# The first group of a Mamba-2 input projection, regrouped by token tile

## The chip, the cores and the metric

The kernel runs on one NeuronCore of a Trainium2 chip. The metric is the device time of one execution in microseconds (us); a time given for a kernel is the median of several runs. A core has five engines that run side by side, each through its own list of instructions in order: TensorE (PE, matrix products and transposes, with results in PSUM), VectorE (DVE), ScalarE (ACT), GpSimd (POOL) and SyncE (SP, which issues the transfers here). They wait for one another through semaphores. The compiler's list of an engine is fixed when the kernel is built, so an instruction that waits holds up everything behind it on its engine.

## The reference, cut to what matters

The kernel computes one step of a decoder trunk of two layers: a Mamba-2 layer (SSD), then a multi-head latent attention layer (MLA), each with a residual, and a final norm. 1024 prompt rows and 8 x 8 sample rows pass through together as T = 1088 rows. Only the entry of the SSD layer matters here:

```python
def rms_norm(x, w):
    xf = x.astype(F32)
    y = xf * lax.rsqrt(jnp.mean(xf * xf, axis=-1, keepdims=True) + NORM_EPS)
    return (y * w.astype(F32)).astype(x.dtype)

def ssd_mixer(h, conv_buf, ssm_state, w_in, conv_w, conv_b, dt_bias, a_log, d_skip, norm_w, w_out):
    proj = jnp.einsum('btd,de->bte', h, w_in)
    z = proj[..., :SSD_D_INNER]
    xbc = proj[..., SSD_D_INNER:SSD_D_INNER + SSD_CONV_DIM]
    dt_raw = proj[..., SSD_D_INNER + SSD_CONV_DIM:]
    xbc, new_buf = causal_conv(xbc, conv_buf, conv_w, conv_b)
    xbc = jax.nn.silu(xbc.astype(F32))
...
    dt = jax.nn.softplus(dt_raw.astype(F32) + dt_bias.astype(F32))
    a_head = -jnp.exp(a_log.astype(F32))
    y, new_state = ssd_scan(xs, dt, a_head, bm, cm, ssm_state.astype(F32))
    y = y + d_skip.astype(F32)[:, None] * xs
    y = y.reshape(b, t, SSD_D_INNER) * jax.nn.silu(z.astype(F32))
```

Here h is the normalised x, z the gate, and xbc holds x, B and C; a norm by group and the product with w_out follow. D_MODEL is 1024, the inner width 2048, and there are 8 groups of 4 heads. Group g needs two columns of 128 for B and C, two of 128 for x, and 256 columns of z; dt has 32 columns for all groups. The decay needs cumulative sums of dt over chunks of 128 rows.

## The kernel before

Products are made from numbers split in two: `split` (line 128) rounds a tile to a high part on ACT and subtracts it on DVE for a low part, and every product is three matmuls, high x high, high x low and low x high. So the rows x are kept normalised and turned as `xh` and `xl` (feature by token), and each weight as `wih` and `wil`.

After a first part for group 0, a loop over the groups g = 1..7 (`ssd_groups`, line 1138) runs 21 steps t per group: a projection piece of group g (`Flow.proj`) beside the scan of group g-1 (`Scan`). In this loop the order on every engine is the order in which the program issues (`manual_schedule`). In the first part before, a scheduler orders the instructions of each engine. The MLA layer behind it is touched by nothing here.

The first part before, `layer_ssd` (lines 1250 to 1309), works so:

- `norm_steps` (line 244) takes the 9 tiles of 128 rows (the last has the 64 sample rows) in three column groups of 384, 384 and 320 rows. `norm_rows` (line 208) loads x, squares it on ACT with a sum per row, takes the root on DVE and POOL (`rstd_of`) and scales the rows on DVE; `norm_cols` (line 229) turns them on PE, and ACT and DVE split them into `xh` and `xl`, with the norm weight as a factor per partition.
- Beside it `Group.pair(0, True)` projects B and C for each column group as its rows come (line 418); then `pair(1)` projects the two x blocks. `Group.block` (line 443) copies each piece to `raw` (two buffers), and convolves the whole block: one ACT instruction (line 466) and three on DVE (line 469).
- `load_zdt` (line 318) loads and splits the weights of z and dt on POOL, and `Group.gates` (line 489) then projects z and dt tile by tile (line 500, 24 matmuls of 288 columns for a tile).
- `ssd_dt` (line 336) makes the decays once dt of all tiles is there: an ACT chain (lines 346 to 348) of |x|, exp and log with table loads between, DVE (350, 352), PE sums (358, 359), transposes (381), and stores to DRAM (388) from where `load_decay` (689) reads the decay rows `M` of a chunk.
- `ssd_groups` then starts with `front(0)` (four PE instructions) and `front1(0)` of the scan, whose ACT work (line 734) waits for `M`. The first matmul of the loop's third projection piece (t = 2 of g = 1) follows `back(0)` of the scan.

SP issues transfers in order; a transfer is issued only when an earlier one on the same of eight semaphores has landed. PSUM has two banks each for the transposes (`tr`) and the projections (`pj`).

Of the kernel before, what the change touches and what calls it, by code (L numbers as in the profile page):

```python
# [9 lines left out]
F32 = mybir.dt.float32  # L10
# [7 lines left out]
D = 1024  # L18
# [126 lines left out]
def ssd_tiles(k):  # L145
# [13 lines left out]
    nc.sync.dma_start(k.alog, k.I["ssd_a_log"][0].partition_broadcast(128))  # L159
    nc.scalar.activation(k.alog, k.alog, AF.Exp)  # L160
# [3 lines left out]
def ssd_consts(k):  # L164
# [7 lines left out]
    nc.sync.dma_start(k.dtb, I["ssd_dt_bias"][0].partition_broadcast(128))  # L172
# [3 lines left out]
def load_vectors(k, vp, psum):  # L176
    nc, I, cp = k.nc, k.I, k.cp
    if True:
        r1 = vp.tile([128, 128], F32, name="r1")
        nc.sync.dma_start(r1, I["ssd_conv_w"].rearrange("o k (b c) -> (o k b) c", c=128))  # L180
        r2 = vp.tile([68, 128], F32, name="r2")
        nc.sync.dma_start(r2[0:16], I["norm_w"].rearrange("l (b c) -> (l b) c", c=128))
        nc.sync.dma_start(r2[16:48], I["ssd_conv_b"].rearrange("o (b c) -> (o b) c", c=128))
        nc.sync.dma_start(r2[48:64], I["ssd_norm_w"].rearrange("o (b c) -> (o b) c", c=128))
        nc.sync.dma_start(r2[64:68], I["mla_q_norm_w"].rearrange("o (b c) -> (o b) c", c=128))
        k.vec = cp.tile([128, 196], F32, name="vec")
        p = psum.tile([128, 512], F32, tag="tr", name="vecp", bufs=PB["tr"])
        nc.tensor.transpose(p[:, :128], r1, k.ident)
        nc.tensor.transpose(p[:, 128:196], r2, k.ident[:68, :68])
        nc.vector.tensor_copy(k.vec, p[:, :196])  # L190
    k.convw = [k.vec[:, 32 * j : 32 * j + 32] for j in range(4)]
    k.normc = [k.vec[:, 128:136], k.vec[:, 136:144]]
    k.convb = k.vec[:, 144:176]
    k.ssdn = k.vec[:, 176:192]
    k.qn = k.vec[:, 192:196]

# [106 lines left out]
def conv_state_T(k, pool, psum):  # L303
    nc, I = k.nc, k.I
    r = k.sqp("cst")[:96]
    src = I["state_conv"].rearrange("o b w c -> (o b w) c")
    for q in range(4):
        nc.sync.dma_start(r[24 * q : 24 * q + 24], src[:, 1024 * q : 1024 * q + 1024])
    for half in range(2):
        p = psum.tile([128, 512], F32, tag="tr", name=f"cvp{half}", bufs=PB["tr"])  # L310
# [5 lines left out]


def load_zdt(k, pool):
    nc = k.nc
    w = k.I["ssd_w_in"][0].rearrange("(k p) e -> p k e", p=128)  # L320
    k.wzd = []
    k.dtr = pool.tile([128, 9, H], F32, name="dtr")
    nc.gpsimd.memset(k.dtr[64:, 8], 0.0)
    for j in range(2):
        ks = slice(4 * j, 4 * j + 4)
        hi = pool.tile([128, 4, 288], F32R, name=f"zdh{j}")
        lo = pool.tile([128, 4, 288], F32R, name=f"zdl{j}")
        raw = load_raw(pool, 4, 288, 1)
        nc.sync.dma_start(raw[:, :, 0:256], w[:, ks, 0:256])
        nc.sync.dma_start(raw[:, :, 256:288], w[:, ks, DIN + CONV :])  # L330
        nc.gpsimd.tensor_copy(hi, raw)
        nc.gpsimd.tensor_tensor(lo, raw, hi.bitcast(F32), op=ALU.subtract)
        k.wzd += kslices((hi, lo), 4)


def ssd_dt(k, pool, psum):
# [5 lines left out]
    alog = k.alog  # L342
    x = k.dtr.rearrange("p i h -> p (i h)")
# [10 lines left out]
    af = a.rearrange("p i h -> p (i h)")  # L354
    pa = psum.tile([128, 512], F32, tag="y", name="dpa", bufs=PB["y"])
    pt = psum.tile([128, 512], F32, tag="pv", name="dpt", bufs=PB["pv"])
    for p, l, ls in ((pa, k.masku, k.masks), (pt, ones, blks)):
        nc.tensor.matmul(p[:, 0:256], l, af[:, 0:256], start=True, stop=True)
        nc.tensor.matmul(p[:, 256:288], ls, af[:64, 256:288], start=True, stop=True)
    acs = pool.tile([128, n], F32, name="acs")  # L360
# [17 lines left out]
    nc.scalar.activation(k.decp, pt[:, :256].rearrange("p (i h) -> p h i", h=H), AF.Exp)  # L378
    p = psum.tile([128, 512], F32, tag="tr", name="acsp", bufs=PB["tr"])
# [2023 lines left out]
```

## Time and profile before

| | |
|---|---|
| time, median of 3 runs | 1993.61 us (1992.71 to 1995.3) |
| the profiled execution's own time | 1994.01 us |
| its span | 1991.9 us |
| mean clock granted to TensorE | 0.979 of full |

The span runs from the first instruction to the last; 2.1 us of the execution's own time lie around it. The profile gives for each engine the busy time; "what ended the idle time" names the instruction or transfer that the engine waited for. In the view by stretches a row has the busy time of each engine in that stretch, the count of instructions in brackets, then the granted clock, the busy share of the transfer engines and GB/s. In the chain of waits a row has start, length, engine, tile and line.

### The profile page before, as it was taken

The numbers are of one execution on the slowest core, as the hardware profiler recorded it, in microseconds if no ns is written. First come the engines' busy times: TensorE is split into PE (matmuls) and PEld (weight loads), VectorE is DVE, ScalarE is ACT, GpSimd is POOL, SyncE is SP. The second block draws the span as 40 slices with busy tenths as digits, with TensorE's granted clock in tenths as the row PEclk, the third lists the DMA queues.
The fourth block names the chain that finished last, engine by engine and source line by source line (L and its number), as shares of the span: only waits on it lengthen the run. The fifth ranks groups of instructions, "written<-read, shape, count | busy, mean of one in ns | idle before, by whom it ended". The sixth has DMA issues, their size and how long they took to land.

```text
span 1991.9 us, 33767 instructions
## 1 busy us (share of the span) xinstructions
PE 1899.0 (95%) x11953; PEld 1739.5 (87%) x11953; DVE 1179.2 (59%) x2551; ACT 1108.6 (56%) x2603; POOL 844.9 (42%) x1142
## 2 busy tenths in 40 slices
PE   6989999999999999799999999999999999889998
PEld 5879999999999999687787999898888888678887
DVE  4516666657575767644524405466787776566665
ACT  5446756666666666744324314334787777655552
POOL 1316463737373748243000001203565556866661
PEclk9989999999999999899999999999999999899999
DMA  4113333323333232634545433232121113554451
GB/s 152 42 31 89 89 99 87 91 87 91 87 94 91 87 93 74 204 135 162 174 162 164 142 136 87 70 106 78 50 69 42 50 43 96 159 162 141 142 153 38
DMA packets 182336, 206.48 MB, mean 104 GB/s; under 512 B 18924, under 2 KB 147832, under 8 KB 181784
## 3 DMA queue, kind: packets, MB, share of 16 engines
q1 hardware_dynamic: 177336, 185.32, 30.4%
q0 software_dynamic: 4752, 18.88, 2.8%
q8 instruction: 95, 1.56, 0.3%
q14 instruction: 73, 0.60, 0.1%
q10 hardware_dynamic: 80, 0.13, 0.0%
HBM read 150.97 MB, written 53.15 MB: 102 GB/s over the span
## 4 chain that ended last, share of the span: by engine, by line
PE 85%; DMA 4%; DVE 4%; ACT 4%; issue 2%; SPq 1%; POOL 0%; POOLq 0%; DVEq 0%; ACTq 0%
PE pj L89 23%; PE pj L101 9%; PE pq L101 5%; PE p L101 5%; PE pob L101 4%; PE poa L101 4%; PE py L759 3%; PE sc L89 2%; PE o L89 2%; PE sc L1704 1%; PE o L1770 1%; PE st L1737 1%; PE o L1769 1%; PE st L1738 1%; PE o L1768 1%
## 5 line engine op out<-in xcount | busy, mean ns | idle before, releaser
L89 PE MATMUL pj<-xh,wih 128*128 128x384 f32 (+1 forms) x768 | 255.0, 336 | 9.3 <-ACT xh L236 4.9
L89 PE MATMUL pj<-xl,wih 128*128 128x384 f32 (+1 forms) x768 | 254.2, 331 | 0.0
L89 PE MATMUL pj<-xh,wil 128*128 128x384 f32 (+1 forms) x768 | 252.6, 329 | 0.0
L1751 POOL TENSOR_TENSOR tl<-P,th 128x384 fp32r<-128x384 f32 (+1 forms) x144 | 133.1, 930 | 132.5 <-ACT P L1749 73.8
L131 DVE TENSOR_TENSOR wil<-wraw,wih 128x512 fp32r<-128x512 f32 x88 | 70.6, 804 | 160.2 <-ACT wih L130 160.1
L89 PEld LDWEIGHTS pj<-xh,wih 128*128 128x128 f32 x768 | 145.8, 191 | 10.9 <-ACT xh L236 5.9
L796 POOL TENSOR_TENSOR y<-y,xD 128x256 f32<-128x256 f32 x64 | 83.8, 1310 | 151.5 <-DVE y L795 141.1
L89 PEld LDWEIGHTS pj<-xl,wih 128*128 128x128 f32 x768 | 146.3, 190 | 0.6
L89 PEld LDWEIGHTS pj<-xh,wil 128*128 128x128 f32 x768 | 145.9, 190 | 0.0
L101 PE MATMUL pj<-wih,xh 128*128 128x256 f32 x504 | 143.4, 288 | 0.0
L101 PE MATMUL pj<-wil,xh 128*128 128x256 f32 (+1 forms) x504 | 139.1, 282 | 0.0
L1748 ACT ACTIVATE th<-st 128x512 fp32r<-128x512 f32 x192 | 94.5, 492 | 68.6 <-PE st L1744 47.1
L617 DVE SCALAR_TENSOR_TENSOR acc<-raw,vec,acc 128x1112 f32<-128x1112 f32 x84 | 130.3, 1551 | 0.2
L101 PE MATMUL pj<-wih,xl 128*128 128x256 f32 x448 | 126.6, 283 | 0.0
L2050 POOL TENSOR_TENSOR kvl<-pgr,kvh 128x256 fp32r<-128x256 f32 x128 | 98.9, 800 | 53.4 <-ACT kvh L2048 53.4
L131 POOL TENSOR_TENSOR xddl<-xdd,xddh 128x256 fp32r<-128x256 f32 x64 | 64.0, 1000 | 116.8 <-ACT xddh L130 116.8
L130 ACT CAST Ch<-acc 128x128 fp32r<-128x128 f32 x56 | 16.9, 302 | 153.7 <-PE py L89 153.7
L734 ACT ACTIVATE M<-M,tok 128x128 f32<-128x128 f32 (+1 forms) x288 | 90.6, 388 | 10.6 <-DMA M<-acs_d 10.5
L101 PEld LDWEIGHTS pj<-wih,xh 128*128 128x128 f32 x504 | 96.1, 191 | 0.0
L1749 ACT ACTIVATE P<-st 128x512 f32<-128x512 f32 x192 | 93.3, 486 | 2.7 <-DVE tl L1751 2.1
L101 PEld LDWEIGHTS pj<-wil,xh 128*128 128x128 f32 (+1 forms) x504 | 93.1, 185 | 0.6
L101 PEld LDWEIGHTS pj<-wih,xl 128*128 128x128 f32 x448 | 85.6, 191 | 0.0
(980 smaller groups left out, 6283.0 us busy)
## 6 DMA issues: line engine op xcount, KB each, us to landing
wraw<-in_ssd_w_in SPq DMA_DIRECT2D x92, 256.0 KB
M<-acs_d SPq DMA_DIRECT2D x64, 256.0 KB
y_d<-xD SPq DMA_DIRECT2D x64, 128.0 KB
s<-in_state_ssm SPq DMA_DIRECT2D x32, 256.0 KB
out_s_ssm<-s SPq DMA_DIRECT2D x32, 256.0 KB
wraw<-in_ssd_w_out SPq DMA_DIRECT2D x16, 512.0 KB
q_d<-qt SPq DMA_DIRECT2D x32, 192.0 KB
qp<-q_d SPq DMA_DIRECT2D x8, 768.0 KB
```

The costliest lines, as they stand in the source:

```text
L89: nc.tensor.matmul(out, a, b, start=(i == 0), stop=(i == n - 1))
L101: nc.tensor.matmul(o, a, b, start=(j == 0), stop=(j == len(ops) - 1))
L131: (eng or nc.vector).tensor_tensor(lo, src, hi.bitcast(F32), op=ALU.subtract)
L617: nc.vector.scalar_tensor_tensor(acc, self.raw[bi][:, j : j + n], k.convw[j][:, blk : blk + 1], acc, op0=ALU.mult, op1=ALU.add)
L734: nc.scalar.activation(M[:m, h, :m], M[:m, h, :m], AF.Relu, bias=c.tk[:, 0, 4 * g + h : 4 * g + h + 1], scale=-1.0)
L759: nc.tensor.matmul(py[:m, h * 64 : h * 64 + 64], c.M[:m, h, :m], c.xdt[:m, h * 64 : h * 64 + 64], start=True, stop=True)
L796: nc.gpsimd.tensor_tensor(y[:m], y[:m], c.xD[:m], op=ALU.add)
L1704: nc.tensor.matmul(ps[:, :n], qh[:96, 128 * i : 128 * i + 128], kh[:96, 512 * c : 512 * c + n], start=True, stop=True)
L1748: nc.scalar.activation(th[:, :n], ps[:, :n], AF.Exp, scale=SCALE)
L1749: nc.scalar.activation(P[:, :n], ps[:, :n], AF.Exp, scale=SCALE)
L1751: eng.tensor_tensor(tl[:, :n], P[:, :n], th[:, :n].bitcast(F32), op=ALU.subtract)
L2050: nc.gpsimd.tensor_tensor(rl[:, r], raw[:, r], rh[:, r].bitcast(F32), op=ALU.subtract)
```

## The change

Group 0 gets a class of its own, `First`, which follows `Flow`, and the first part is put under the program's own order, like the loop.

- Rows are normalised, turned, split and projected tile by tile. The norm weight is no longer a factor per partition in the split: one row of it is spread over 128 partitions by two matmuls with ones (`nw`), and one DVE instruction scales a tile's rows by root and weight.
- The gate and dt projection of a tile follows as soon as it is turned. The z and dt weights come in four parts, split on ACT and DVE.
- B, C and the two x blocks follow as 12 projection pieces. Steps of the dt chain (now a generator, `ssd_dt`) lie between the pieces. The convolution of a block is issued at the next block's first piece; the last block is convolved in two halves.
- The vectors and the convolution state are loaded and turned inside the tile loop; `exp` of `a_log` moves into the dt chain; the store of the convolution rows moves into the first steps of g = 1.

```diff
+class First(Flow):
+    def begin(self):
+        self.load_x(0)
+        for q in range(4):
+            self.load_z(q)
+        row = self.rp.tile([128, RAW], F32, tag="raw", name="nrow", bufs=2)[0:1, :D]
+        nc.sync.dma_start(row, k.I["norm_w"][0:1])
+        nc.sync.dma_start(k.dtb, k.I["ssd_dt_bias"][0].partition_broadcast(128))
+        for i in range(1, 4):
+            self.load_x(i)
...
+        self.square(0)
+        self.root(0)
+        for hf in range(2):
+            c = slice(512 * hf, 512 * hf + 512)
+            p = self.psum.tile([128, 512], F32, tag=("y", "pv")[hf], name=f"nwp{hf}", bufs=1)
+            nc.tensor.matmul(p, ones, row[:, c], start=True, stop=True)
+            nc.vector.tensor_copy(self.nw[:, c], p)
+        self.scale(0)
+        self.turn(0)
+    def scale(self, i):
+        x = self.xt[i]
+        self.k.nc.vector.scalar_tensor_tensor(x[:m], x[:m], self.rs[:m, i : i + 1], self.nw[:m], op0=ALU.mult, op1=ALU.mult)
+    def split_z(self, q):
+        hi, lo = (self.zd.tile([128, 2, 288], F32R, name=f"zd{x}{q}") for x in "hl")
+        split(self.k, hi, lo, self.zraw[q])
+        self.wz += kslices((hi, lo), 2)
+    def turn(self, i):
+        m, x = TILES[i][1], self.xt[i]
+        self.p[i] = []
+        for q in range(2):
+            p = self.psum.tile([128, 512], F32, tag="tr", name=f"xtp{i}_{q}", bufs=PB["tr"])
+            for a in range(4):
+                d = 4 * q + a
+                self.k.nc.tensor.transpose(p[:, a * 128 : a * 128 + m], x[:m, d * 128 : d * 128 + 128], self.k.ident[:m, :m])
+            self.p[i].append(p)
+    def take(self, i):
+        k, (t0, m) = self.k, TILES[i]
+        for q, p in enumerate(self.p.pop(i)):
+            s = (slice(None), slice(4 * q, 4 * q + 4), slice(t0, t0 + m))
+            split(k, k.xh[s], k.xl[s], p.rearrange("p (a t) -> p a t", a=4)[:, :, :m])
+        if m == 64:
+            k.nc.gpsimd.tensor_copy(k.xh[:, :, T:], k.xl[:, :, SEQ:].bitcast(F32))
+    def gate(self, i):
+        k, nc, m = self.k, self.k.nc, TILES[i][1]
+        if i % 3 == 0:
+            self.z.append(self.gp.tile([128, 3, 256], F32, tag="z", name=f"z0{i}", bufs=4))
+        z = self.z[i // 3]
+        p = self.psum.tile([128, 512], F32, tag="pj", name=f"pz{i}", bufs=PB["pj"])
+        drain(mm_tok(nc, p, m, 288, [(*both(k.xh, k.xl, i, kk), *self.wz[kk]) for kk in range(8)]))
+        def ev():
+            if m == 64:
+                fold(nc, z[:, i % 3], p, 256)
+            else:
+                nc.scalar.copy(z[:m, i % 3], p[:m, :256])
+            nc.vector.tensor_tensor(k.dtr[:m, i], p[:m, 256:288], k.dtb[:m], op=ALU.add)
+            if m == 64:
+                nc.vector.tensor_tensor(k.dtr[:m, i], k.dtr[:m, i], p[64:128, 256:288], op=ALU.add)
+        return ev
+    def norm(self, vectors, states):
+        self.begin()
+        self.split_z(0)
+        self.split_z(1)
+        self.take(0)
+        self.split_z(2)
+        self.split_z(3)
+        for i in (1, 2):
+            self.square(i)
+            self.root(i)
+        self.scale(1)
+        self.turn(1)
+        for n in range(1, 10):
+            ev = self.gate(n - 1)
+            if n < 9:
+                self.take(n)
+            if n + 2 < 9:
+                self.square(n + 2)
+                self.root(n + 2)
+            if n + 1 < 9:
+                self.scale(n + 1)
+            if n + 3 < 9:
+                self.load_x(n + 3)
+            if n == 2:
+                ssd_consts(self.k)
+            if n in (2, 6):
+                next(vectors)
+            if n in (3, 7):
+                next(states)
+            if n in (5, 6):
+                self.load(n - 5)
+            if n in (8, 9):
+                self.split(n - 8)
+                self.load(n - 6)
+            if n + 1 < 9:
+                self.turn(n + 1)
+            ev()
+    def blocks(self, dt, nxt, scan_of):
+        for t in range(12):
+            bi, ci = divmod(t, 3)
+            ev = self.proj(t)
+            if t < 9 and ci < 2:
+                p = 2 * bi + 2 + ci
+                self.split(p)
+                if p < 6:
+                    self.load(p + 2)
+                else:
+                    nxt.load(p - 6)
+            if t in (9, 10):
+                nxt.split(t - 9)
+                nxt.load(t - 7)
...
+            if t >= 3 and ci == 0:
+                self.tails(bi - 1)
+                self.conv(bi - 1, slice(0, n))
+            if t == 0:
+                for z in self.z[:2]:
+                    nc.scalar.activation(z, z, AF.Silu)
+                z = self.z[2]
+                nc.scalar.activation(z[:, :2], z[:, :2], AF.Silu)
+                nc.scalar.activation(z[:64, 2], z[:64, 2], AF.Silu)
+            if t < 8:
+                next(dt)
+            if t == 8:
+                scan = scan_of()
+                scan.load_decay(0)
+                self.silu(0, slice(0, SEQ))
+            if t == 11:
+                self.conv(3, slice(0, 512))
+                self.silu(1, slice(0, 512))
+            ev()
+            if ci == 2 and t < 11:
+                self.conv0(bi)
+            if t == 10:
+                self.conv0(3, slice(0, 512))
+        self.conv0(3, slice(512, n))
+        self.conv(3, slice(512, n))
+        self.tails(3)
+        scan.front(0)
+        self.silu(1, slice(512, SEQ))
+        scan.front1(0)
 def ssd_dt(k, pool, psum):
...
+    yield
+    nc.scalar.activation(alog, alog, AF.Exp)
     nc.scalar.activation(u, x, AF.Abs)
     nc.scalar.activation(u, u, AF.Exp, scale=-1.0)
     nc.scalar.activation(u, u, AF.Ln, bias=ones[:, 0:1])
...
+    yield
     pa = psum.tile([128, 512], F32, tag="y", name="dpa", bufs=PB["y"])
...
+    yield
     acs = pool.tile([128, n], F32, name="acs")
     nc.vector.tensor_copy(acs, pa[:, :n])
...
 def layer_ssd(k):
-            norm_steps(k, x_loader(k), None, k.xh, k.xl, p0, psum, [st0], XB, before, after)
-        for _ in range(6):
-            next(st0)
-            load_zdt(k, p0)
-            for _ in st0:
-                pass
-            ssd_dt(k, p0, psum)
+        with tc.manual_schedule(engines={e.engine for e in (nc.tensor, nc.vector, nc.scalar, nc.gpsimd, nc.sync)}):
+                first = First(k, pools, zd, x0)
+                first.norm(load_vectors(k, x0, psum), conv_state_T(k, rp, psum))
...
+            scan = first.blocks(ssd_dt(k, dtp, psum), f1, scan_of)
+            ssd_groups(k, first, scan, f1, pools, sps[0], psum, st, left, right, als)
```

296 lines of the change are left out of this document (119 added, 177 removed).

## The prediction

> **What bounds the kernel now.** I read the page first: the span, the engines, the slices and the chain that ended last.
>
> ```profile
> span 1991.9 us, 33767 instructions
> PE 1899.0 (95%) x11953; PEld 1739.5 (87%) x11953; DVE 1179.2 (59%) x2551; ACT 1108.6 (56%) x2603; POOL 844.9 (42%) x1142
> PE   6989999999999999799999999999999999889998
> PE 85%; DMA 4%; DVE 4%; ACT 4%; issue 2%; SPq 1%; POOL 0%; POOLq 0%; DVEq 0%; ACTq 0%
> ```
>
> TensorE is busy for 95% of the span and holds 85% of the chain. The first slice of 40 is the poorest in PE. So I read the stretches of the part that the diff touches, and one row of the loop behind it.
>
> ```profile
> 0.00:9.34 9.34, 0.00 (x0) 0.00 (x0) 0.00 (x0) 4.05 (x7) 0.56 (x10) 1.00 0.68 216
> 9.34:18.05 8.71, 2.81 (x8) 1.23 (x8) 5.03 (x10) 5.04 (x10) 1.46 (x2) 1.00 0.91 280
> 18.05:57.23 39.18, 37.01 (x218) 32.59 (x218) 19.32 (x34) 20.44 (x40) 7.17 (x13) 1.00 0.30 88
> 57.23:70.64 13.41, 9.08 (x53) 8.48 (x51) 11.28 (x7) 4.86 (x10) 8.10 (x9) 0.94 0.23 62
> 70.64:88.61 17.97, 17.97 (x98) 17.97 (x99) 7.03 (x5) 7.01 (x10) 5.08 (x7) 0.86 0.17 47
> 88.61:116.57 27.96, 27.93 (x210) 27.66 (x209) 6.19 (x12) 9.13 (x16) 0.33 (x2) 1.00 0.01 3
> 116.57:124.15 7.58, 0.00 (x0) 0.00 (x1) 1.72 (x6) 6.97 (x9) 0.48 (x1) 0.74 0.00 0
> 124.15:130.35 6.20, 6.20 (x20) 4.22 (x21) 2.33 (x6) 1.85 (x6) 1.15 (x4) 0.50 0.07 20
> 130.35:142.08 11.73, 11.03 (x57) 10.58 (x56) 2.33 (x6) 4.26 (x13) 1.65 (x3) 0.85 0.13 29
> 142.08:143.42 1.34, 1.34 (x11) 1.34 (x12) 1.22 (x4) 0.39 (x3) 1.18 (x2) 1.00 0.93 274
> 143.42:500.00 356.58, 356.12 (x2613) 350.95 (x2613) 234.51 (x449) 228.16 (x611) 201.68 (x300) 1.00 0.31 91
> ```
>
> From 143.42 on, where the third projection of group 1 starts, PE is busy for 356.12 of 356.58 us at full clock: there the kernel is bound by PE work, so what this start wins or loses goes through to the end. Before 143.42, PE stands for 15.2 us until 18.05, 4.3 us of 57.23:70.64 and the whole of 116.57:124.15, and after the last two the granted clock is down to 0.86 and 0.50. The chain names what these wait for, and gives the pace of PE where it runs:
>
> ```profile
> 44.49 0.42 PE xtp L235 x3
> 64.34 3.07 DVE wil L131
> 70.64 17.97 PE pj L89 x96
> 95.22 21.32 PE pz L101 x160
> 121.28 1.28 ACT L348
> 124.15 1.22 PE dpa L358 x2
> 125.37 0.56 PE dpa L359 x2
> 134.98 3.26 DMA M<-acs_d
> 142.58 0.84 PE py L759 x8
> 143.42 3.57 PE pj L89 x24
> 147.54 4.19 PE pj L89 x24
> ```
>
> The hole near 64 is a weight split of 3.07 us on DVE between the convolutions. The hole after 116.57 is the dt chain: it starts only when the last gate tile is projected, holds three table loads like that at 121.28, then its PE sums run at half clock, and the decay rows come back from DRAM at 138.24 while the loop has only two projections to run.
>
> **The change, part by part.** I add up the time at which the same matmul (third projection of group 1, now 143.42) will start. PE's pieces at full clock: a gate tile 24 x 21.32/160 = 3.2 us, a turn of a tile 8 x 0.42/3 = 1.1, a projection piece 4.2 (384 columns) or 3.6 (320). The other engines' pieces:
>
> ```profile
> L130 ACT CAST sh<-s0p 128x512 fp32r<-128x512 f32 x4 | 2.3, 585 | 0.1
> L131 DVE TENSOR_TENSOR sl<-s0p,sh 128x512 fp32r<-128x512 f32 x4 | 2.7, 684 | 0.0
> L220 ACT ACTIVATE sq<-xt 128x1024 f32<-128x1024 f32 x8 | 8.4, 1057 | 6.2 <-DMA xt<-in_x_prompt 6.0
> L220 ACT ACTIVATION_READ_ACCUMULATOR sq<-xt 128x1 f32 x8 | 1.5, 191 | 0.0
> L1124 DVE SCALAR_TENSOR_TENSOR wol<-wraw,vec,woh 128x1024 fp32r<-128x1024 f32 x16 | 20.4, 1302 | 17.8 <-ACT woh L1117 17.8
> L130 ACT CAST wih<-wraw 128x512 fp32r<-128x512 f32 x25 | 15.2, 615 | 5.2 <-DMA wraw<-in_ssd_w_in 4.0 <-PE pj L101 1.1
> L205 POOL TENSOR_TENSOR rs<-rs,nhalf 128x3 f32<-128x3 f32 x3 | 3.1, 1042 | 24.2 <-ACT wih L130 9.8 <-DVE rs L200 8.5 <-PE xtp L235 6.0
> L512 ACT ACTIVATE z<-z 128x768 f32<-128x768 f32 x2 | 1.7, 847 | 0.1
> L453 ACT COPY raw<-pj 128x384 f32<-128x384 f32 x8 | 3.5, 478 | 14.9 <-DVE acc L469 8.6 <-PE pj L89 6.3
> L469 DVE SCALAR_TENSOR_TENSOR acc<-raw,vec,acc x12: 1362/1376/2643, 59.4 to 93.4; 128x1112 f32<-128x1112 f32 x12
> 1.19 0.42 SPq L159 DMA_DIRECT2D alog<-in_ssd_a_log  x1
> 6.44 1.06 ACT L220 ACTIVATE sq<-xt 128x1024 f32<-128x1024 f32 x1 [1.24 <-DMA xt<-in_x_prompt]
> ```
>
> *Start, to the first gate matmul.* SP now issues x of tile 0, then eight transfers for z and dt (1.18 MB), the row of the norm weight, the bias, then tiles 1 to 5. A transfer waits for the landing of the eighth before it, so the row waits for the first z part and lies behind the others. By 216 GB/s of 0:9.34 the 1.77 MB ahead of it have come by 8.2 us. Taken the other way, the last z part waits for x of tile 0 (6.44 today, 6.0 without the 0.42 of the alog load ahead) and needs a landing like that of M, 3.26: 9.3. I take 10.0 for the row, with 8.2 and 13 as ends. No matmul of one row on 512 columns is in the trace; the nearest is the 256-column one at 124.15, 1.22 at half clock, so two take about 4.0 (2.4 if it counts by instruction, 4.9 by columns). Then in one chain: copy of the second half 0.7, scale 1.3 (16.0), four transposes at half clock 0.6, two roundings 1.2, the two late z splits on ACT 1.4, two squares of 1.25 (DVE asks for the roots of tiles 1 and 2 ahead of the scale of tile 1), root 0.2, scale 1.3, the turn of tile 1 at half clock 2.3: 25.4 with the hand-overs (ends 22 and 29). PE stands for 5.8 us within that.
>
> *Tiles.* The first gate finds a half clock: 3.8, then a turn, 30.3. After it a tile's step is the longer of PE's work, 3.2 + 1.1 = 4.3, and a circle through ACT and DVE: four transposes 0.6, two roundings 1.2, square 1.25, scale 1.3, with the root and five hand-overs 0.3: 4.6. So 4.6 (ends 4.3, and 5.2 if half of POOL's root, 1.04, falls into the circle). Five steps give 53.3, the vector turns 0.3, the step with the convolution state's eight turns 5.2, the last full gate 3.2, the sample tile (16 matmuls) 2.1: 64.1. The z copy, dt sum and split of the low parts are under PE's 4.3: DVE carries 2 x 0.68 + 1.3 + 0.4 a tile, ACT 2 x 0.59 + 1.25 + 0.4.
>
> *Blocks.* Twelve pieces, 4 x (2 x 4.19 + 3.57) = 47.8. Into them go the dt chain's PE bits, now at full clock: half of 2 x (1.22 + 0.56), with transposes and sums for the sample states 2.8 in all. The 7.6 us of 116.57:124.15 vanish from the path if ACT keeps up. From the start of the first piece ACT must do a z copy, two weight splits, three table loads (one for SiLU), four SiLUs, two evictions and the dt functions: 0.4 + 1.2 + 3.8 + 2.8 + 1.0 + 1.7 = 10.9, and DVE two steps of 0.5; PE comes to the dt sums after 12.0. So 0.1 us of cover is left; if it is gone, PE pays one for one. Convolutions, 3 x 1.38 a block against 12 us of PE, stay hidden, and POOL no longer splits weights beside DVE, so the 3.07 us has no cause. Decay rows are loaded four pieces ahead of their use, so the 3.26 is hidden. End of the pieces: 64.1 + 47.8 + 2.8 = 114.7.
>
> *Into the loop.* The scan's front needs the first half of x's last block through copy, convolution and SiLU, about 0.9 us after the last piece by the rows above halved. Then front 0.8, piece 4.2, front 0.8, piece 4.2, a wait of 0.2 for the state input and 1.34 as in 142.08:143.42: 127.1. The convolution rows' four transposes and copies, and six store issues on SP ahead of a decay load in g = 1, move from the first part into a stretch where SP has slack; I cost them at 0.4 in the allowance below.
>
> *Allowance.* Twelve ordered queues meet at more places than I have followed. I add 2.0 us (ends 0 and 5): 129.1.
>
> **Sum.** 143.4 - 129.1 = 14.3 us less. Against the profiled execution's own 1994.01 (span 1991.9 and 2.1 around) that is 1979.7; the median of the runs, 1993.61, is 0.4 lower, so 1979.3.
>
> **The rivals.**
>
> *ACT holds the blocks.* The cover of 0.1 us for the dt sums is gone, because the third weight part is loaded only when the first is split and lands 3.3 later, or a table load more stands in the way; the gates' circle comes out at 5.2. For it: ACT's 6.97 busy of 7.58 in 116.57:124.15, three table loads long. Against: POOL and DVE are freer than now. It costs 3 in the blocks and 4 in the tiles: about 1986.
>
> *The tiles run at half clock* (the slower side). The turns break PE's matmuls in each tile, after a stand of 5.8 us. If the clock stays at 0.50 as in 124.15:130.35, a step is 2 x 4.3 = 8.6, and eight steps cost 8 x 4.0 = 32 more: 2011. It decides from a step of 4.6 + 14.3/8 = 6.4 us on, that is a granted clock of 0.68 or less through the tiles. Against: 18.05:57.23 holds nearly all of the 9 x 8 transposes between matmuls (44.49 is one place), at clock 1.00; and in 70.64:88.61, which follows a stand, the mean of 0.86 is some 5 us at half clock and full clock for the rest.
> The Trainium skill says in "TensorE: Matmul & The Clock Gate", Part 4: PE-mode transpose, that a PE transpose does not count as busy for the gate in the same way. By that rule this rival would come true; the row 18.05:57.23 says that matmuls between the turns are enough.
>
> *Nothing comes through.* The time is lost again later, since the loop's first groups would wait for stores or states that the old gap let through. The row 143.42:500 with 0.46 us idle speaks against it; 1993.6.
>
> **How the numbers follow.** Forecast 0.68 (own range 1972 to 1985), ACT 0.18 (1982 to 1990), half clock 0.08, nothing 0.06. A measurement of this kernel tells 0.2%, 4 us, from no change. Under 1989.6 lie the forecast and nearly all of ACT's case: faster 0.86; same 0.06; slower 0.08. The range: all low ends (start 22, step 4.3, no allowance) give 1979.3 - 3.4 - 1.7 - 2.0 = 1972; all high ends (start 29, seven steps of 5.2, allowance 5) 1979.3 + 3.6 + 4.2 + 3.0 = 1990. 1972 to 1990 leaves the two last cases out.
>
> **What would show it.** First gate matmul at 25 us (22 to 29); gate tiles 4.6 apart at clock 1.00 from the second on; first projection piece at 64; no idle of PE over 1 us from there to the loop; the dt sums 12 us after the first piece with no wait; the third projection of group 1 at 127 to 131; the time from there to the end unchanged, 1848.5. A clock under 0.7 in the tiles, a step over 5.2, or PE waiting for the dt functions would make the prediction wrong, and an unchanged span with a shorter start would show the third rival.

## The result, and the profile after

| | before | after |
|---|---|---|
| time, median of four runs each | 1994.41 us (1992.71 to 1995.3) | 1978.18 us (1977.12 to 1981.1) |
| ratio, with 95% interval | 1 | 0.9922 (0.9905 to 0.9939) |
| span of the profiled execution | 1991.9 us | 1976.7 us |
| start of the marker, the third projection of group 1 | 143.42 us | 126.08 us |
| from the marker to the end | 1848.5 us | 1850.6 us |

The changed kernel is faster by 0.78%, 1.1 us under the forecast of 1979.3. The page after, the lines that answer to those shown of before:

```profile
span 1976.7 us, 33806 instructions
PE 1890.7 (96%) x11957; PEld 1733.9 (88%) x11957; DVE 1185.7 (60%) x2564; ACT 1108.4 (56%) x2604; POOL 835.6 (42%) x1139
PE   6999999999999999799999999999999999789998
```

Nearly all of the difference lies ahead of the marker. That stretch, first of before and then of after (start and end, length, then busy us of PE, PEld, DVE, ACT and POOL with instruction counts, the granted clock, DMA share, GB/s):

```profile
0.00:143.42 143.42, 113.37 (x667) 104.08 (x668) 56.44 (x86) 64.01 (x117) 27.16 (x51) 0.93 0.25 73
```

```profile
0.00:126.08 126.08, 106.09 (x672) 100.15 (x673) 61.33 (x98) 64.68 (x120) 21.24 (x50) 1.00 0.29 85
0.00:9.26 9.26, 0.00 (x0) 0.03 (x1) 0.15 (x1) 3.56 (x5) 1.17 (x9) 1.00 0.69 195
9.26:24.14 14.88, 7.31 (x21) 4.32 (x21) 8.24 (x12) 4.87 (x9) 2.08 (x2) 1.00 0.62 220
24.14:60.92 36.78, 36.49 (x277) 35.44 (x276) 23.35 (x42) 18.09 (x38) 10.80 (x12) 1.00 0.23 57
60.92:108.16 47.24, 47.24 (x282) 45.85 (x281) 21.17 (x28) 26.75 (x44) 3.34 (x18) 1.00 0.21 55
108.16:126.08 17.92, 15.06 (x99) 14.51 (x99) 8.41 (x15) 11.39 (x25) 3.86 (x9) 1.00 0.18 49
```

TensorE stands at the start (16.8 us until 24.14), hardly in the tiles and the blocks, and 2.9 us ahead of the marker. The 17.3 us at the marker have two halves. TensorE stood for 143.42 - 113.37 = 30.05 us before and for 126.08 - 106.09 = 19.99 after: 10.1 less. And it was busy for 7.3 us less with nearly the same instructions; the clock granted over the stretch rose from 0.93 to 1.00, which by an estimate is worth 0.07 x 113.37 = 7.9. So a little under half of the gain is not a wait that went away but the slow clock that followed two of the waits.

The chain after, from the first gates to the marker (start, us, what):

```profile
22.55 1.94 PE xtp L625 x8
24.48 3.94 PE pz L101 x24
...
29.30 3.21 PE pz L101 x24
...
33.62 3.21 PE pz L101 x24
36.83 0.06 issue
36.89 1.06 PE xtp L625 x8
...
60.92 11.85 PE pj L89 x72
72.77 0.43 PE dpa L345 x2
...
91.92 16.24 PE pj L89 x96
...
126.08 3.52 PE pj L89 x24
```

The tiles are 33.62 - 29.30 = 4.32 us apart (4.33 later on), and all of it is PE but for some 0.06 us ahead of each turn. The dt sums come 11.85 us after the start of the first projection piece, straight behind the matmuls of the first three pieces. Eleven pieces are done at 91.92 + 16.24 = 108.16, the twelfth takes PE to about 111.65, and then two waits are left, which the timeline names (in brackets the idle time and what ended it):

```profile
113.08 0.33 PE L809 MATMUL trp<-ident,acc 128*128 128x128 f32 x1 [1.43 <-ACT acc L710]
...
119.79 0.49 PE L814 MATMUL cb<-acc 128*128 128x128 f32 x2 [1.44 <-DVE cbm L833]
```

### The profile page after: what moved, and what is told of

Read it like the earlier page. It is cut to its first block, busy times and chain, and to the rows that moved or that the text cites. A ratio compares the mean times of both kernels' runs of the same rounds, so it can differ in the third digit from the quotient of the medians.

```text
span 1976.7 us, 33806 instructions
## 1 busy us (share of the span) xinstructions
PE 1890.7 (96%) x11957; PEld 1733.9 (88%) x11957; DVE 1185.7 (60%) x2564; ACT 1108.4 (56%) x2604; POOL 835.6 (42%) x1139
## 4 chain that ended last, share of the span: by engine, by line
PE 78%; POOL 7%; issue 4%; DVE 4%; DMA 4%; ACT 3%; SPq 0%; POOLq 0%; DVEq 0%; ACTq 0%
PE pj L89 24%; PE pj L101 9%; PE pq L101 6%; PE pob L101 4%; PE poa L101 4%; POOL kvl L2139 4%; PE py L865 3%; PE sc L1793 2%; PE st L1826 1%; PE o L1859 1%; PE st L1827 1%; PE pz L101 1%; PE st L1828 1%; PE o L1858 1%; PE o L1857 1%
```

## The experiments

All start from the changed kernel but for one, which starts from the kernel before. Behind the marker the profiled executions took between 1848.5 and 1852.2 us, all kernels together; so differences of a few us are read at the marker, and the medians carry only the larger ones. They come from several chips, on which the kernel before took 1994.41 (the result), 1995.75, 1996.45 and 1995.79 us; each ratio is to the kernel before on the same chip, so ratios compare better than medians. "First piece" is the start of the first projection piece of group 0. In five executions with the same instructions up to there it came between 60.52 and 61.81, so what lies behind it is compared from the first piece to the marker.

| run | first piece | marker | to the end | median | ratio to before (95%) |
|---|---|---|---|---|---|
| changed kernel | 60.92 | 126.08 | 1850.6 | 1978.18 | 0.9922 (0.9905 to 0.9939) |
| dt chain last | 60.52 | 138.04 | 1849.1 | 1989.25 | 0.9967 (0.9955 to 0.998) |
| turns three times | 76.51 | 141.67 | 1851.7 | 1995.68 | 1.0003 (0.9992 to 1.0013) |
| squares twice | 67.32 | 132.49 | 1851.4 | 1983.27 | 0.9935 (0.9919 to 0.9952) |
| before, no splits on POOL | | 143.49 | 1850.8 | 1995.33 | 1.0 (0.9989 to 1.001) |
| dt functions later | 61.81 | 127.80 | 1850.6 | 1978.96 | 0.9915 (0.9895 to 0.9934) |
| front first | 60.99 | 125.89 | 1851.5 | 1978.41 | 0.9911 (0.9895 to 0.9928) |
| front first, SiLU late | 61.47 | 124.94 | 1852.2 | 1977.14 | 0.9901 (0.9881 to 0.9921) |
| new start | 57.00 | 122.19 | 1848.9 | 1973.68 | 0.9892 (0.9875 to 0.9908) |
| start, squares up | 57.71 | 122.87 | 1851.2 | 1975.39 | 0.9893 (0.9876 to 0.9909) |
| start, squares up, PE kept busy | 55.08 | 120.24 | 1850.2 | 1972.59 | 0.9884 (0.9867 to 0.99) |
| start, x early | 52.40 | 117.56 | 1850.1 | 1970.60 | 0.9879 (0.9863 to 0.9896) |
| x early and front first, SiLU late | 53.92 | 117.41 | 1850.2 | 1969.02 | 0.9865 (0.9848 to 0.9881) |

### Where the gain comes from: the dt chain put back

```diff
-            if t < 8:
-                next(dt)
             if t == 8:
-                scan = scan_of()
-                scan.load_decay(0)
                 self.silu(0, slice(0, SEQ))
...
         self.tails(3)
+        drain(dt)
+        scan = scan_of()
+        scan.load_decay(0)
         scan.front(0)
```

> Theory A (the gain comes from laying the dt chain beside the blocks: its wait on ScalarE, its sums at half clock and its way through DRAM): with the dt chain put back behind the twelve pieces, TensorE waits again some 8 us for the dt functions, then runs its sums and the first front at a granted clock near 0.5. The third projection of group 1 starts at 135 us (133 to 137) instead of 126.08, and the whole takes 1985 to 1989 us. Theory B (the gain comes from the gates' place and from the weight split hole near 64 us that is gone; the dt chain is short of work to hide either way): the marker moves by less than 3 us, and the whole stays under 1982.

The marker moved to 138.04, a little beyond theory A's range, and the median to 1989.25; B is out. The timeline and the windows of this run, from the last pieces on:

```profile
115.97 1.22 PE L345 MATMUL dpa<-dta,masku 128*128 128x256 f32 x2 [8.02 <-DVE dta L338]
```

```profile
115.97:119.50 3.53, 3.53 (x9) 2.10 (x10) 0.46 (x1) 0.26 (x1) 1.13 (x5) 0.50 0.00 0
119.50:138.04 18.54, 16.17 (x82) 14.89 (x83) 5.33 (x14) 9.94 (x22) 3.76 (x10) 0.77 0.19 53
```

TensorE waits 8.02 us for the dt functions, runs their sums at a clock of 0.50 and the first projections of the loop at 0.77. From the first piece to the marker it is 77.5 us instead of 65.2. So 12 of the 17.3 us at the marker come from where the dt chain stands (with the decay rows that follow it), and the rest, about 5, from the start, the tiles and the blocks together. These 5 were not taken apart further but for the next run.

### The hole of before near 64 us

In the kernel before, the z, dt and x weights of group 0 are split on ScalarE and VectorE:

```diff
-        nc.gpsimd.tensor_copy(hi, raw)
-        nc.gpsimd.tensor_tensor(lo, raw, hi.bitcast(F32), op=ALU.subtract)
+        split(k, hi, lo, raw)
...
-                          k.nc.gpsimd if g == 0 and bi > 1 else None)
+                          None)
```

> The kernel before, with the low parts of the z, dt and x weights of group 0 split on VectorE and ScalarE rather than GpSimd. Theory A (the hole near 64 us, 4.3 us of TensorE standing and the lower clock after it, comes from the splits on GpSimd beside VectorE: 3.07 us for a subtraction that takes 0.68 elsewhere): the long subtraction falls below 1 us, TensorE stands for less than 1.5 us between 57 and 71, the third projection of group 1 starts at 137 to 140 instead of 143.42, the whole 3 to 6 us shorter than before. Theory B (the hole is VectorE's own queue of convolutions and the engine of the split is no matter): the hole stays over 3 us and the whole within 1.5 us of before.

Both theories are half right. The long subtraction is gone, first before and then in this run (the timeline of VectorE):

```profile
64.27 3.15 DVE L131 TENSOR_TENSOR wil<-wraw,wih 128x512 fp32r<-128x512 f32 x1
```

```profile
62.91 0.69 DVE L131 TENSOR_TENSOR wil<-wraw,wih 128x512 fp32r<-128x512 f32 x1 [1.85 <-ACT wih L130]
```

So the splits on GpSimd did stretch it: in the trace of the kernel before, one of them ran beside it from 63.13 to 66.87, and the long subtraction ended 0.55 us after that. But the time did not come back:

```profile
18.05:57.23 39.18, 34.46 (x186) 30.37 (x187) 18.19 (x32) 18.34 (x37) 2.17 (x5) 0.96 0.22 66
57.23:70.64 13.41, 12.54 (x76) 11.79 (x75) 9.24 (x11) 7.78 (x14) 2.14 (x9) 1.00 0.56 144
70.64:88.61 17.97, 16.86 (x106) 16.51 (x105) 10.02 (x9) 8.48 (x12) 3.41 (x6) 1.00 0.14 35
```

TensorE stands 4.7 + 0.9 + 1.1 = 6.7 us in these three stretches, against 2.2 + 4.3 + 0 = 6.5 before, and the marker is 143.49 against 143.42. The standing moved forward: there is now a wait of 2.15 us ahead of 28.68, for VectorE's low part of a tile's rows, which the kernel before does not have. Why the scheduler's order came out so was not followed; changing the engine of the split alone was worth nothing here.

### What sets the tile's step

*Turns three times.* Each transpose of `turn` is run three times into the same place.

```diff
-                self.k.nc.tensor.transpose(p[:, a * 128 : a * 128 + m], x[:m, d * 128 : d * 128 + 128], self.k.ident[:m, :m])
+                for _ in range(3):
+                    self.k.nc.tensor.transpose(p[:, a * 128 : a * 128 + m], x[:m, d * 128 : d * 128 + 128], self.k.ident[:m, :m])
```

> Each of the 72 transposes of the tiles is run three times into the same place. Theory A (turns and matmuls together hold the clock, and TensorE sets the tile step): step 4.33 + 2 x 1.06 = 6.45 us at granted clock 1.00, first projection piece near 83 (two turns at half clock add 7.8, seven at full clock 14.9), the whole near 2001. Rule of the Trainium skill, 'TensorE: Matmul & The Clock Gate', Part 4: PE-mode transpose (a transpose does not count as busy in the same way): with half of TensorE's time in transposes the clock falls towards 0.5, a step takes 9 to 13 us, and the whole is above 2020.

```profile
24.69 4.68 PE xtp L626 x24
29.37 3.21 PE pz L101 x24
32.59 2.81 PE xtp L626 x24
```

```profile
27.00:28.00 1.00, 1.00 (x7) 1.00 (x6) 0.00 (x0) 0.48 (x1) 0.00 (x0) 0.50 0.00 0
28.00:29.00 1.00, 1.00 (x9) 1.00 (x8) 0.69 (x1) 0.10 (x1) 0.00 (x0) 0.73 0.00 0
```

A step is 2.81 + 3.21 = 6.02 us, TensorE is never idle in it, and the matmuls run at full pace; the 16 more transposes cost 1.75 us rather than 2.12, 0.117 us each in a row of 24 against 0.133 in a row of 8. The first piece came at 76.51 rather than near 83 and the total at 1995.7, 5 under theory A: its mechanism held, its size was too large. The rule of the Trainium skill ("TensorE: Matmul & The Clock Gate", Part 4: PE-mode transpose) does not hold in this run. The first row is a run of transposes alone, behind 5.39 us in which TensorE stood. The granted clock rises within it (0.50, then 0.73 in these two windows), and the gate behind it starts at full pace, where in the changed kernel the gate behind 8 transposes starts at half pace (3.94). Transposes alone lifted the clock.

*Squares twice.* The square of tiles 3 to 8 is issued a second time.

```diff
             if n + 2 < 9:
                 self.square(n + 2)
+                self.square(n + 2)
```

> The square of tiles 3 to 8 is run twice on ScalarE (1.06 + 0.19 us more in each). Theory A (the circle turn, rounding, square, root, scale, turn takes about 4.1 us and lies just under TensorE's 4.33): steps of 5.1 to 5.4 us with TensorE waiting 0.8 to 1.1 in each of six tiles, the first projection piece at 66 to 67 instead of 60.92, the whole 5 to 6 us longer. Theory B (ScalarE has room in the tiles, the circle is far below TensorE's time): no more than 1 us.

The chain of this run in a tile:

```profile
29.37 1.07 ACT xh L130 x2
30.45 1.06 ACT sq L608 x2
31.52 1.16 ACT sq L608 x2
32.79 1.28 DVE xt L616
34.22 0.65 PE xtp L625 x4
34.89 1.07 ACT xh L130 x2
```

The circle of the forecast sets the step: turn, rounding, square, root, scale, turn, 5.52 us from one `xh` to the next (29.37 to 34.89), and the first piece moves by 6.4, both just over theory A's ranges. The second square starts 1.19 us after the first (30.33 and 31.52 in the timeline); without it the circle takes 4.33, which is the step of the changed kernel. So it sets the step there too: in both kernels the turn starts 0.15 us after the scale ends (34.07 and 34.22 here; 36.74 and 36.89 in the changed kernel):

```profile
35.46 1.28 DVE L616 SCALAR_TENSOR_TENSOR xt<-xt,rs,nw 128x1024 f32<-128x1024 f32 x1
```

TensorE's own work is 3.21 + 1.06 = 4.27, and the 0.06 of "issue" in the chain of the changed kernel is its room. Theory A holds in its effect, but the circle does not lie under TensorE's time; it is the longer of the two by 0.06. It is a circle of queues: the scale of a tile does not need the square that it follows, which is the next tile's; it only stands behind the first step of that tile's root on VectorE.

### The cover of the dt functions

```diff
+            if t == 1:
+                for z in self.z[:2]:
+                    nc.scalar.copy(z, z)
             if t < 8:
                 next(dt)
```

> Two copies in place of 128x768 (about 0.8 us each) are put on ScalarE between the first projection piece and the dt functions. Theory A (the dt functions end 0.8 us before TensorE asks for them, so the blocks had that much cover and no more): TensorE waits 0.6 to 1.1 us ahead of the dt sums, and the third projection of group 1 starts 0.6 to 1.2 us later than 126.08. Theory B (the sums would be late for another engine first, or ScalarE has more room): no wait of over 0.3 us ahead of the sums.

```profile
74.20 0.70 PE L345 MATMUL dpa<-dta,masku 128*128 128x256 f32 x2 [0.58 <-DVE dta L338]
```

Theory A, for the kernel with two copies more on ScalarE: a wait of 0.58, just under its range, and 0.27 more in the sums themselves (0.70 against 0.43); first piece to marker grew by 66.0 - 65.2 = 0.8. The functions ended 12.4 us after the first piece instead of 10.9, 1.5 later, of which 0.58 reached TensorE: the cover was 0.9 us.

### The entry into the loop

*Front first.*

```diff
+        scan.front(0)
+        scan.front1(0)
         self.conv0(3, slice(512, n))
         self.conv(3, slice(512, n))
         self.tails(3)
-        scan.front(0)
         self.silu(1, slice(512, SEQ))
-        scan.front1(0)
```

> The front of the scan's first tile (its four PE operations, and the copies, products and ReLUs behind them) is issued ahead of the second half of x's last convolution. Theory A (TensorE waits 1.44 us ahead of the second front because the masked product that frees the one bank stands behind that half convolution in VectorE's queue): that wait falls below 0.3, the third projection of group 1 starts at 124.6 us (124 to 125.3) instead of 126.08, the whole 1 to 2 us shorter than 1978. Theory B (the work that is pushed back is due just as soon): a wait of the same size shows at another place before the marker or at the fifth tile, and the whole moves by less than 0.5 us.

Theory B. The wait on `cbm` was gone and another had come in its place (chain of this run):

```profile
118.02 0.85 DVE acc L696
...
118.89 1.07 ACT acc L710
...
120.83 1.28 ACT L846
122.12 0.63 ACT M L846
...
123.13 0.94 POOL xddl L131
...
124.11 0.50 PE st L89 x2
```

ScalarE's SiLU of the second half (L710) waits in its queue for VectorE's convolution, and behind it stand the exponential of the decay rows (L846, a table load of 1.28 ahead of it) and the split for the state product `st`. The SiLU itself is wanted only several tiles later.

*SiLU late.* The same, and the SiLU of the second half goes behind the loop's first projection:

```diff
         self.tails(3)
-        self.silu(1, slice(512, SEQ))
...
     def state_out(self, t, scan):
+        if t == 0:
+            self.silu(1, slice(512, SEQ))
```

> As the run with the front of the first tile issued first, and the SiLU of the second half of x moved behind the first projection of group 1. Theory A (in that run ScalarE stood still for the half convolution ahead of this SiLU, and the exponential of the decay rows, the split of x and TensorE's state product stood behind it: the wait had only moved): the wait of 1.4 us is gone from both places and the third projection of group 1 starts at 124.6 (124.2 to 125.2) instead of 125.89. Theory B (the state product is late for another cause, the decay rows' exponential with its table load or the split on GpSimd): the marker stays within 0.4 us of 125.89. The whole moves by 1.5 us at most, about what two profiled executions differ by behind the marker, so the marker decides.

```profile
119.13 4.19 PE pj L89 x24
123.31 0.35 PE st L89 x3
```

Theory A: the state product follows the second projection at once, the marker is at 124.94, and from the first piece it is 63.5 us instead of 65.2. Only the 1.42 us ahead of the first front are left. The price is two table loads more on ScalarE (1.28 each, at 119.85 and 126.04), for which TensorE did not wait up to 130 us.

### The start

*New start.* The norm row is loaded behind x of tile 0, all z splits are ahead of the rounding of tile 0, tile 1 is squared and scaled without waiting for tile 2, and its turn lies inside the first gate.

```diff
         self.load_x(0)
+        row = self.rp.tile([128, RAW], F32, tag="raw", name="nrow", bufs=2)[0:1, :D]
+        nc.sync.dma_start(row, k.I["norm_w"][0:1])
         for q in range(4):
             self.load_z(q)
-        row = self.rp.tile([128, RAW], F32, tag="raw", name="nrow", bufs=2)[0:1, :D]
-        nc.sync.dma_start(row, k.I["norm_w"][0:1])
...
         self.square(0)
         self.root(0)
+        self.split_z(0)
...
+        if i == 0:
+            for _ in range(16):
+                next(mm)
+            self.turn(1)
+        drain(mm)
...
-        self.split_z(0)
-        self.split_z(1)
+        for q in range(1, 4):
+            self.split_z(q)
         self.take(0)
-        self.split_z(2)
-        self.split_z(3)
-        for i in (1, 2):
-            self.square(i)
-            self.root(i)
+        self.square(1)
+        self.root(1)
         self.scale(1)
-        self.turn(1)
...
+            if n == 1:
+                self.square(2)
+                self.root(2)
+                self.scale(2)
...
```

> The row of the norm weight is loaded right behind x of tile 0, all four z splits are ahead of the rounding of tile 0, the scale of tile 1 no longer waits for the root of tile 2, and the turn of tile 1 lies inside the first gate. Theory A (the start is set by a chain: the row's landing at 9.26, and the splits, squares and roots that are ahead of the scale of tile 1 in the queues): first gate matmul at 15 (14 to 17) instead of 24.14, third projection of group 1 at 118 (116 to 121), the whole 6 to 10 us shorter than 1978. Theory B (the start is set by transfers: z and x have to come in, 216 GB/s over the first 9 us): the first gate not before 20, the tiles behind it waiting for x, the whole less than 4 us shorter.

The first gate matmul came at 13.80, yet the marker gained only 3.9 us. The second gate waited until 24.43, since the squares of tiles 1 and 2 now stood behind the roundings of tiles 0 and 1 in ScalarE's queue (14.49 and 19.55). Neither theory saw this.

*Squares up.* Against the new start:

```diff
+        for i in (1, 2):
+            self.square(i)
+            self.root(i)
         self.take(0)
-        self.square(1)
-        self.root(1)
         self.scale(1)
...
             if n == 1:
-                self.square(2)
-                self.root(2)
                 self.scale(2)
```

> As the run with the new start, but with the squares and roots of tiles 1 and 2 ahead of the rounding of tile 0, and the scale of tile 2 ahead of the square of tile 3. Theory A (in that run the second gate waited until 24.43 for squares that stood behind the roundings in ScalarE's queue): the second gate starts at 20 (19 to 21), no half clock after it, the first projection piece at 52.5, the third projection of group 1 at 117.5 (116 to 119.5), the whole 3.5 to 6 us shorter than that run's 1973.7. Theory B (x of tiles 1 and 2 lands too late for it): the squares wait for their transfers until 14 or more, and the marker stays above 120.5.

Theory B, its 14 us missed by a little: x of tile 1 was late.

```profile
13.86 1.06 ACT L609 ACTIVATE sq<-xt 128x1024 f32<-128x1024 f32 x1 [4.26 <-DMA xt<-in_x_prompt]
```

The square waits 4.26 us for its transfer, and with it the rounding of tile 0 behind it: the first gate slips to 16.87. The marker is at 122.87, no earlier than with the new start alone.

*PE kept busy.* To that, five matmuls of 512 columns on a constant, two ahead of the broadcast of the norm row and three behind it.

```diff
+        self.warm(2)
         for hf in range(2):
...
         self.scale(0)
+        self.warm(3)
         self.turn(0)
+
+    def warm(self, n):
+        for _ in range(n):
+            self.k.nc.tensor.matmul(self.wp_, self.wt[:, :128], self.wt, start=True, stop=True)
```

> As the run before it in this list, with five matmuls of 512 columns on a constant in TensorE's idle time: two ahead of the broadcast of the norm row, three behind it; their results are not used. Theory A (the granted clock follows how TensorE was occupied just before, so the broadcast, the first turn and the first gate run at half clock because TensorE stood): the broadcast takes 2 us instead of 3.74, the turn of tile 0 1.1 instead of 1.97, the first gate's matmuls 134 ns apart from the start, and the third projection of group 1 comes 2 to 4 us earlier than in the run without them. Theory B (the chain of ScalarE and VectorE through splits, squares and scales sets the start, so a faster TensorE only waits longer): less than 1 us.

The marker comes 2.6 us earlier, but not all for A's reason: the broadcast still took 3.78 us, and only the turn (1.04) and the gate behind it ran at full pace. About 1.1 of the 2.6 belong to x of tile 1, which landed earlier in this execution: its square started at 12.79 against 13.86. The rest, 1.6, is the faster pace: from the first gate to the second it is 7.64 us (15.81 to 23.45) instead of 9.21 (16.87 to 26.08).

*X early.* x of tile 1 is loaded between the z parts and x of tile 2 behind them; the norm row lies in a tile of 128 rows, 127 of them zero; its copies are ahead of the root, and `square(1)` is between the z splits; two matmuls on a constant on either side of the broadcast.

```diff
+        row = self.rp.tile([128, RAW], F32, tag="raw", name="nrow", bufs=2)[:, :D]
+        nc.gpsimd.memset(row, 0.0)
         self.load_x(0)
...
+        self.load_z(0)
+        nc.sync.dma_start(row[0:1], k.I["norm_w"][0:1])
+        self.load_z(1)
+        self.load_x(1)
+        self.load_z(2)
+        self.load_z(3)
+        self.load_x(2)
...
```

> The start once more: x of tile 1 is loaded between the z parts and x of tile 2 right behind them, the norm row is broadcast by a matmul over 128 rows of which 127 are zero, between matmuls on a constant that are not used, its copies come ahead of the root, and the square of tile 1 between the z splits. Theory A (with the squares moved up, x of tile 1, which landed at 13.8, was the start's limit because four more tiles of x shared the transfers with it): the square of tile 1 starts before 10.5, the first gate at 12 (11 to 13.5), the second gate at 18 (17 to 20), the third projection of group 1 at 115 (113.5 to 117). Theory B (z and the x tiles come in at a fixed rate, so an earlier x makes z later): the first gate waits for the z splits until 15 or more and the marker stays above 118.

The square of tile 1 starts at 9.48, the first gate at 12.53, the marker is at 117.56: theory A, half a us past its range, since the second gate (20.77) missed its time. Several things changed at once here, so the time of the square shows that x of tile 1 came earlier, but the gain at the marker is not that of the loads alone. The turn ahead of the second gate waits for the scale of tile 2, whose root was there at 16.29, but which stands behind the subtraction of tile 1 (17.08 to 18.37) in VectorE's queue (timeline; the releaser that the second row names is the next instruction there):

```profile
18.29 1.28 DVE L629 SCALAR_TENSOR_TENSOR xt<-xt,rs,nw 128x1024 f32<-128x1024 f32 x1
...
19.71 1.06 PE L638 MATMUL xtp<-ident,xt 128*128 128x128 f32 x8 [1.79 <-DVE rs L199]
```

*Both.* The start of the run with x early and the entry of the run with SiLU late, in one kernel.

> The two runs before it in this list in one kernel. If TensorE's work sets the time from the marker on, what they win at the marker adds up and goes through: third projection of group 1 at 113.5 (112 to 116), the whole 11 to 14 us shorter than the changed kernel's 1978.2, a ratio to the kernel before near 0.986. Rival (the loop's first groups cannot start earlier, since weights, stores or the decay rows are then late): the marker is reached, but 3 us or more come back behind it, and the ratio stays above 0.9875.

1969.02 us, 0.9865 of before (0.9848 to 0.9881): faster than both kernels. The marker is at 117.41, not 113.5, and the whole is 9.2 us shorter than the changed kernel by the medians, 11 by the ratios. The entry gave its 1.7 (63.5 from the first piece), but the start was 1.5 later than in the run before it with the same instructions, because the clock rose later (below). Nothing came back behind the marker: 1850.2.

## Why the prediction was right

- **Gain goes through from the marker on.** Held in all runs: the marker moved between 117.4 and 143.5, and the time behind it stayed within 1848.5 to 1852.2 without following it.
- **Start, 25.4.** 24.14. The norm row landed at 9.26 instead of 10.0 and its two matmuls took 3.75 instead of 4.0. That a chain of queues sets it and not the transfers is right for this order; with the queues reordered, x of tile 1 became the limit. (The terms of the forecast add up to 25.5 even without the hand-overs, so 25.4 was a little short.)
- **Tiles, 4.6.** The mechanism was right: the circle sets the step, not TensorE's 4.27. Its size was off, 4.33 measured. The forecast added whole durations; in the trace consecutive instructions of one engine overlap by some 0.1 us each, and the two roundings cost 0.96 instead of 1.2. The five steps gained 1.7 us by this, the step with the convolution state's turns another 0.7 (4.50 against 5.2), and the first and the last gates gave 0.5 back. With the start's 1.3, this makes the first piece 60.92 instead of 64.1. The rival of half clock had its deciding quantities, the step and the clock, at 4.33 and 1.00; the tripled turns show that the transposes do not hold the clock down, but lift it.
- **Blocks, 47.8 + 2.8.** From 60.92 to 111.65 it is 50.7, against 50.6. No wait at the dt sums; their cover was 0.9 us and not 0.1. The rival of ScalarE holding the blocks fell by that much.
- **Into the loop, 12.4 us behind the last piece.** 14.4. Here the forecast missed something: the second front waits 1.44 us for the one bank of `cb`, which `cbm(0)` frees. That product stands behind the second half convolution on VectorE (until 117.02) and, through the copies that it follows, behind that half's SiLU on ScalarE (until 118.12); it ran at 119.54. The first wait was 1.43 rather than 0.9. Both are over the 1 us that the forecast allowed TensorE to stand. The allowance of 2.0 was there for such a place and came to the right size. That was luck as to the place: no step named it.
- **Sum.** 129.1 - 126.08 = 3.0: the start gives 1.3, the tiles 1.9, the blocks nothing, and the entry's 2.0 used up the allowance. The marker lies 0.9 us ahead of the 127 to 131 that the forecast gave as its sign, most of it from the tiles.
- **Behind the marker, 1848.5 unchanged.** 1850.6. With 1849.1 and 1848.9 in kernels that differ from the changed one only ahead of the marker, and 1850.8 in the kernel before without splits on GpSimd, this is no more than one execution differs from another by. It hid 2 of the 3 us: with the measured marker in its place the forecast's sum gives 1976.3. That the total came out within 1.1 us was luck to that extent.
- **Cause.** The place of the dt chain is worth 12 of the 17.3 us, part of them clock. The other 5 are the start, the tiles and the blocks, and what each gave is not shown. The forecast's reason for the other hole, subtractions stretched by GpSimd, is true of the subtraction, but removing it in the old order gained nothing.

## What to carry to other kernels

A chain of small functions on another engine is cheap beside long matmuls and dear behind them, where it is paid twice: in the wait and in the slow clock after it. An instruction that is not urgent but waits for another engine holds up the urgent one behind it in its queue; moving the front one alone only moves the wait, so follow the queue to the next consumer before costing an order at nothing. And when two circles are nearly as long, as TensorE's 4.27 and the other engines' 4.33 here, making the longer one shorter is worth at most the difference; making either longer costs nearly all that is added.

## What the runs showed of the hardware

The moment at which the clock rises is not fixed by the program. In kernels with the same instructions up to there, the first gate took 3.94, 4.08, 4.15, 4.68, 4.88 and 4.99 us (3.2 at full pace). The last two kernels of the table have the same start, and one broadcast the row at full pace, the other at half (timeline, first the run with x early, then both):

```profile
1.36 3.66 PE L588 MATMUL warmp<-warmt 128*128 128x512 f32 x4 [1.36 <-POOL warmt L566]
6.00 1.95 PE L596 MATMUL nwp<-nrow,warmt 128*128 128x512 f32 x4 [0.97 <-DMA nrow<-in_norm_w]
```

```profile
1.36 3.78 PE L588 MATMUL warmp<-warmt 128*128 128x512 f32 x4 [1.36 <-POOL warmt L566]
5.70 3.75 PE L596 MATMUL nwp<-nrow,warmt 128*128 128x512 f32 x4 [0.56 <-DMA nrow<-in_norm_w]
```

Between 1.36 and 9.24 the second was busy but for 0.56 us and still at half pace, 7.9 us; the first was at full pace after 4.6, with a pause of 0.97 in them. In the run with PE kept busy it took longer still, though TensorE had no pause from 1.36 on; 3.78 us of its work was the broadcast of one row. Of this work the last six instructions

```profile
8.78 4.98 PE L599 MATMUL warmp<-warmt 128*128 128x512 f32 x6
```

took 0.83 us each, nearer to half pace (3.78 for four) than to full (1.88 for four).

The Trainium skill ("TensorE: Matmul & The Clock Gate", Part 1: The HAM clock gate) says that the window of 3.4 us runs freely, so that the moment varies. The variation agrees with it, but two windows, an estimate of 6.8 us from that page, would be its most, and 7.9 is longer. Whether the pause, the zeros in the row or its single row matter was not tried. At the start of the span the granted clock is no guide either: it stands at 1.00 in the window 9.26:24.14 of the changed kernel, where the turn at 22.55 takes 1.94 us against 1.06 for the later ones, so there the pace has to be read from the durations.
